# Mixer A's queries and keys: token tiles multiplied as they lie, blocks ordered after the rotary embedding, whole rows stored

## The chip, the core and the metric

The program runs on one core of a Trainium2 chip. The metric is the device time of one execution in microseconds (us), as the median of several runs. PE is the matrix engine (TensorE), DVE the vector engine, ACT the scalar engine, POOL is GpSimd, and SP issues most of the DMA transfers. Each engine works through its own instructions in a fixed order that was set when the program was built; an instruction that waits holds up everything behind it on its engine.

## What is computed

One decoder layer over 2048 tokens of width 1024. The part that matters here makes the rotated queries and keys of mixer A:

```python
h = rmsnorm(x, g_attn[l])
proj = jnp.einsum('bsd,de->bse', h, w_in[l]) + b_in[l]
qa, ka, va, qb, kb, vb = jnp.split(proj, splits, axis=-1)
...
def sliding_window_sink_gqa(q, k, v, sinks):
    S = q.shape[1]
    q, k = rope(q, S), rope(k, S)
    o, _ = banded_attention(q.transpose(0, 2, 1, 3), k.transpose(0, 2, 1, 3),
                            v.transpose(0, 2, 1, 3), WINDOW_A - 1, sinks=sinks)
```

`qa` has 8 heads of 64 (512 columns), `ka` 2 heads (128 columns): five column tiles of 128. `rope` multiplies each feature by the cosine of its token's angle and adds its partner feature, 32 places away, times the sine. Mixer A then attends in blocks of 128 neighbouring tokens. Mixer B attends to the same normalised input with other projections and needs a bias table for each of its 8 heads; behind both come the output projection and a gated feed-forward network.

## The kernel before

The kernel holds the normalised input transposed in SBUF, as two parts that sum to it (`hh` and the rest `hl`), features on partitions and tokens along the row. The tokens lie sorted by their remainder modulo 16: column `n` of `hh` is a token of remainder class `n // 128`, and the 128 places in a class run in steps of 16 tokens. Mixer B wants that order. Mixer A wants blocks of neighbouring tokens.

`project` works in three stretches. First it normalises the input and makes the values (to about 148 us of the profiled execution). Then, in lines 280 to 314, it makes mixer A's queries and keys: for each of five column tiles `c` (0 to 3 queries, 4 the keys) and four token tiles `t` of 512, `gemm` issues 24 matmuls into one PSUM bank (8 chunks of features by 3 products of parts). These 20 units are called groups here, g0 to g19 in the order in which they run, and the stretch the rotary stretch. With `natural=True`, line 174 picks the 512 tokens of four blocks out of `hh`: 64 pieces of 8 neighbouring elements each, the pieces 128 elements apart. Third come mixer A's attention and mixer B's projections, interleaved; these call `gemm` with `natural=False`, which reads 512 neighbouring elements.

What follows a group's matmuls is a chain over three engines. Lines 300 to 303 copy the four quarters of the bank, crosswise, into `t1`, by turns on DVE (L303) and ACT (L301), each waiting for the one before; L305 (DVE) adds the bias and multiplies by the cosine, the last to read the bank; L306 (DVE) does the same with the sine; L307 (POOL) adds; L309 (ACT) and L310 (DVE) split the sum into two parts `hia`; line 311 stores it as two DMAs from SP, one for each head. `t1`, `t2` and `hia` have two buffers each.

Between these stand mixer B's bias tables (`bias_tables`), two steps for each of eight heads. `rows` multiplies three small matmuls into PSUM (L381), copies them out on ACT (L382, tile `lt`, two buffers) and stores them (L383, `Ls`). `table` loads them back skewed (L387, L389, L392: `tt`, `n4`, and four loads for `n1`), reorders them on DVE (L393, L394) and stores the table (L396, `Ts`). `tt`, `n4` and `n1` have one buffer each.

PSUM has 8 banks, and all results of the rotary stretch, those of `gemm` and the three of each `rows`, share one ring of them (`ps2`, 8 buffers).

The order of the instructions on every engine is made by a scheduler when the kernel is built: it goes by the data, the buffers and its own estimate of durations. A buffer or an address that is used again makes the new user wait for the last one. After the rotary stretch its SBUF pools are freed, and the tiles of the third stretch (the masks, keys, queries, scores `t`, probabilities `p` and transposed probabilities `hl` of mixer A, `hi` of mixer B's projections) lie on the same addresses.

Of the kernel before, what the change touches and what calls it, by code (L numbers as in the profile page):

```python
# [43 lines left out]
def shape_constants():  # L44
# [3 lines left out]
    res = np.array(RES)  # L48
    tok = (n // 128) * 128 + (n % 8) * 16 + res[(n % 128) // 8]
    ang = tok.astype(np.float32)[None, :] * inv[:, None]  # L50
# [97 lines left out]
def project(tc, es, ident, half, x, g_attn, w_in, b_in, sinks, rel, rope, mask_a, onehot, sc):  # L148
# [18 lines left out]

    def gemm(ps, w, t, natural, tag="mm"):
        acc = ps.tile([P, 512], F32, tag=tag, name="acc")
        n = 0  # L170
        for k in range(KC):
            for a, h in ((w[0], hh), (w[0], hl), (w[1], hh)):
                if natural:
                    mv = h[:, k, :].rearrange("p (r jj j a) -> p jj j r a", r=16, jj=4, j=4)[:, t]
                else:
                    mv = h[:, k, t * 512:(t + 1) * 512]
                nc.tensor.matmul(acc, a[:, k, :], mv, start=(n == 0), stop=(n == 3 * KC - 1))  # L177
                n += 1
        return acc
# [100 lines left out]
    with ExitStack() as ex:  # L280
        ps = ex.enter_context(tc.tile_pool(name="ps2", bufs=8, space=PSUM, reuse_waits="tile"))
        rp = ex.enter_context(tc.tile_pool(name="r1", bufs=2, reuse_waits="tile"))
        rc = ex.enter_context(tc.tile_pool(name="r2", bufs=1, reuse_waits="tile"))
# [7 lines left out]
        bias = bias_tables(tc, ex, ps, rel, onehot, sc)  # L291
        for c in range(5):
            w = load_w(c * P)
            for t in range(NT):
                cols = slice(t * 512, (t + 1) * 512)
                acc = gemm(ps, w, t, True)
                t1 = rp.tile([P, 512], F32, tag="t1", name="t1")
                for q4 in range(4):
                    d, s4 = t1[q4 * 32:(q4 + 1) * 32, :], acc[(q4 ^ 1) * 32:((q4 ^ 1) + 1) * 32, :]
                    if q4 % 2:  # L300
                        nc.scalar.copy(d, s4)  # L301
                    else:
                        nc.vector.tensor_copy(d, s4)  # L303
                t2 = rp.tile([P, 512], F32, tag="t2", name="t2")
                nc.vector.scalar_tensor_tensor(t2, acc, bcol[:, c:c + 1], tab[:, 0, cols], op0=ALU.add, op1=ALU.mult)  # L305
                nc.vector.scalar_tensor_tensor(t1, t1, bsw[:, c:c + 1], tab[:, 1, cols], op0=ALU.add, op1=ALU.mult)  # L306
                nc.gpsimd.tensor_add(t2, t2, t1)  # L307
                hi = rp.tile([P, 2, 512], F32R, tag="hi", name="hia")
                nc.scalar.copy(hi[:, 0], t2)  # L309
                nc.vector.tensor_sub(hi[:, 1], t2, hi[:, 0].bitcast(F32))  # L310
                store_heads(sc.qA if c < 4 else sc.kA, 2 * c if c < 4 else 0, hi, cols)
                n = c * NT + t - 2
                if 0 <= n < 2 * NH:
                    bias(n // NH, n % NH)


    with ExitStack() as ex:
# [5 lines left out]
        def proj_b(todo, ps=ps, tag="mm"):  # L323
            nonlocal w
            for c0, c, t in todo:
                if t == 0:
                    w = load_w(c0 + c * P)
                bc = bcol[:, c0 // P + c:c0 // P + c + 1]
                acc = gemm(ps, w, t, False, tag)
                hi = ev.tile([P, 2, 512], F32R, tag="hi", name="hi")  # L330
# [17 lines left out]
def bias_tables(tc, es, ps, rel, onehot, sc):  # L348
# [15 lines left out]
    for b in range(3):  # L364
        o32 = bw.tile([P, 384], F32, tag="lt", name="o32")
        nc.sync.dma_start(o32, onehot[:, b, :])
# [8 lines left out]
    def rows(h):  # L375
        lw = bw.tile([P, P], F32R, tag="lw", name="lw")
        nc.vector.tensor_scalar(out=lw, in0=ones, scalar1=rhi[:, h:h + 1].bitcast(F32), scalar2=None, op0=ALU.mult)
        lt = bw.tile([P, 3, 384], F32, tag="lt", name="lt")
        for b in range(3):
# [917 lines left out]
```

## Time and profile before

| | us |
|---|---|
| median of 3 runs | 2406.85 (2405.19 to 2408.16) |
| the profiled execution | 2404.51 |
| its span on the core | 2402.7 |
| PE busy in it | 2300.4 (96%) |
| DVE busy | 1604.5 (67%) |
| ACT busy | 1054.1 (44%) |

In the rotary stretch and up to the first matmuls of attention (about 148 to 304 us) PE is without a pause but for the waits shown in the rows; the granted clock of PE is 1.00 of full speed there. The chain that ended last is PE for 51% of the span. In the views, a row of an engine gives the idle time before an instruction or a group of them and what ended it. SPq rows are the issuing of DMAs; the transfers themselves run later.

### The profile page before, as it was taken

What the parts mean: (1) busy time and instruction counts of PE and PEld (TensorE: products, weight loads), DVE (VectorE), ACT (ScalarE), POOL (GpSimd) and SP (SyncE); (2) the same over time, 40 slices, a digit from 0 to 9 for tenths busy, and PEclk for the clock granted to TensorE, in tenths of its full rate; (3) what the DMA queues carried; (4) which work ended last, traced back from release to release, by engine and by line L of the source; (5) the groups of instructions that cost most, each with busy time, mean ns of one, the idle gap of its engine ahead of it and who ended that gap; (6) DMA issues with size and microseconds to landing.
All of it is one profiled execution on the core that took longest, in us unless ns stands there. A gap on an engine that the chain in (4) does not pass through costs nothing.

```text
span 2402.7 us, 33903 instructions
## 1 busy us (share of the span) xinstructions
PE 2300.4 (96%) x11765; PEld 1947.0 (81%) x11765; DVE 1604.5 (67%) x3151; ACT 1054.1 (44%) x2371; POOL 468.1 (19%) x418
## 2 busy tenths in 40 slices
PE   7999999997999889897999999899999999999998
PEld 7987788886999878785888888678888878888887
DVE  5335655447999977668877776786666746557555
ACT  5323355453898862336332323342332324444442
POOL 2211211111111010113232232423232330000000
PEclk9999999998999999998999999999999999999999
DMA  7666566659988687755544544333232339768651
GB/s 220 202 189 215 159 188 173 165 157 239 222 222 219 174 244 199 241 171 203 196 155 148 175 149 167 127 127 110 91 120 92 106 115 399 240 198 283 205 189 71
DMA packets 284156, 436.21 MB, mean 182 GB/s; under 512 B 24448, under 2 KB 153088, under 8 KB 278480
## 3 DMA queue, kind: packets, MB, share of 16 engines
q1 hardware_dynamic: 279968, 423.41, 57.5%
q0 software_dynamic: 3728, 10.30, 1.5%
q8 instruction: 93, 1.52, 0.3%
q14 instruction: 79, 0.65, 0.1%
q10 hardware_dynamic: 288, 0.33, 0.0%
HBM read 286.50 MB, written 147.46 MB: 181 GB/s over the span
## 4 chain that ended last, share of the span: by engine, by line
PE 51%; DVE 5%; DMA 4%; issue 1%; POOL 0%; ACT 0%; SPq 0%; DVEq 0%; POOLq 0%; ACTq 0%
PE bY L1225 7%; PE Yu L1031 7%; PE Yg L1031 6%; PE bZ L1225 5%; PE bX L1225 5%; PE Xu L1031 4%; PE Zu L1031 4%; PE Zg L1031 4%; PE Xg L1031 4%; PE acco L893 3%; DMA ob<-oB 1%; DVE wl L998 1%; DMA draw<-in_w_down_dram 1%; DVE xs L915 1%; DMA hraw<-hT 0%
## 5 line engine op out<-in xcount | busy, mean ns | idle before, releaser
L1178 DVE TENSOR_TENSOR o<-r,o 128x1024 fp32r<-128x1024 f32 x154 | 191.2, 1252 | 131.9 <-ACT o L1177 124.1
L1177 ACT CAST o<-r 128x1024 fp32r<-128x1024 f32 x154 | 162.2, 1054 | 225.0 <-DMA r<-in_w_down_dram 50.8
L996 ACT CAST wh<-T 128x512 fp32r<-128x512 f32 x176 | 107.2, 621 | 250.1 <-PE Yu L1031 80.5
L1125 POOL TENSOR_TENSOR c<-c,c 128x512 f32<-128x512 f32 x66 | 105.2, 1594 | 567.9 <-DVE c L1049 389.4
L476 DVE TENSOR_TENSOR hl<-pt,hl 128x512 fp32r<-128x512 f32 (+1 forms) x224 | 145.6, 657 | 81.9 <-ACT hl L475 81.4
L451 ACT ACTIVATE p<-t,m 128x256 f32<-128x256 f32 (+1 forms) x384 | 177.4, 480 | 18.0 <-DVE m L676 18.0
L1225 PE MATMUL bY<-o 128*128 128x512 f32 x792 | 180.5, 389 | 0.0
L1225 PEld LDWEIGHTS bY<-o 128*128 128x128 f32 x792 | 148.6, 188 | 30.9
L177 PE MATMUL acc<-hh,wh 128*128 128x512 f32 x416 | 170.0, 409 | 0.7 <-DVE vt L247 0.7
L177 PE MATMUL acc<-hh,wl 128*128 128x512 f32 x416 | 170.4, 410 | 0.0
L177 PE MATMUL acc<-hl,wh 128*128 128x512 f32 x416 | 169.9, 408 | 0.0
L893 PE MATMUL acco<-woh,oT 128*128 128x512 f32 x512 | 163.4, 397 | 3.7 <-ACT oT L864 3.4
L998 DVE TENSOR_TENSOR wl<-T,wh 128x512 fp32r<-128x512 f32 x176 | 153.2, 882 | 0.3
L494 PE MATMUL o<-hl,v 128*128 128x128 f32 (+1 forms) x816 | 141.8, 294 | 7.2 <-DVE hl L476 5.8
L475 ACT CAST hl<-pt 128x512 fp32r<-128x512 f32 (+1 forms) x224 | 125.3, 569 | 45.2 <-PE pt L470 44.9
L429 PE MATMUL s<-k,q 128*128 128x256 f32 (+1 forms) x768 | 122.1, 290 | 18.7 <-DMA k<-kB 8.8
L470 PE MATMUL pt<-ident,p 128*128 128x128 f32 x848 | 133.7, 279 | 4.8 <-DVE hl L476 2.4
L429 PEld LDWEIGHTS s<-k,q 128*128 128x128 f32 x768 | 100.6, 191 | 26.8 <-DVE nma L566 7.4
L1225 PE MATMUL bX<-o 128*128 128x512 f32 x528 | 120.6, 389 | 1.1 <-DVE o L1178 1.1
L494 PEld LDWEIGHTS o<-hl,v 128*128 128x128 f32 x816 | 111.5, 193 | 12.4 <-DVE hl L476 9.6
L1225 PE MATMUL bZ<-o 128*128 128x512 f32 x528 | 120.3, 389 | 0.0
L893 PEld LDWEIGHTS acco<-woh,oT 128*128 128x128 f32 x512 | 96.8, 189 | 25.4 <-ACT oT L864 4.1
(465 smaller groups left out, 5801.3 us busy)
## 6 DMA issues: line engine op xcount, KB each, us to landing
r<-actS SPq DMA_DIRECT2D x154, 256.0 KB
actS<-c SPq DMA_DIRECT2D x128, 256.0 KB
wraw_g<-in_w_gate_dram SPq DMA_DIRECT2D x44, 512.0 KB
wraw_u<-in_w_up_dram SPq DMA_DIRECT2D x44, 512.0 KB
r<-wT SPq DMA_DIRECT2D x88, 256.0 KB
r<-in_w_down_dram SPq DMA_DIRECT2D x66, 256.0 KB
k<-kB SPq DMA_DIRECT2D x32, 512.0 KB
draw<-in_w_down_dram SPq DMA_DIRECT2D x22, 512.0 KB
```

The source lines that it names most:

```text
L177: nc.tensor.matmul(acc, a[:, k, :], mv, start=(n == 0), stop=(n == 3 * KC - 1))
L429: nc.tensor.matmul(s[:, i, :n], b["q"], b["k"][m], start=(m == 0), stop=(m == 1))
L451: nc.scalar.activation(b["pv"](p[:, i, :n]), b["tv"](b["t"]), AF.Exp, scale=-1.0, bias=nm[:, c:c + 1], accum_out=l[:, c:c + 1])
L470: nc.tensor.transpose(pt[:, sl, :], p[:, i, hfn * P:(hfn + 1) * P], ident)
L476: nc.vector.tensor_sub(lo, pt[:, a:z, :], hi.bitcast(F32))
L494: nc.tensor.matmul(out, v[:, vi, :], mov, start=(first and n == 1), stop=(last and n == 2 * len(jobs)))
L893: nc.tensor.matmul(acc, oT[kk // 2][:, kk % 2, a, i * P:(i + 1) * P], b[:, kk, :], start=(n == 0), stop=(n == 11))
L998: nc.vector.tensor_sub(lo, src, hi.bitcast(F32))
L1031: nc.tensor.matmul(bank, a[:, k], b[:, k], start=(first and m == 0), stop=(m == 11), skip_group_check=not first)
L1177: nc.scalar.copy(o[:, 0], r)
L1178: V.tensor_sub(o[:, 1], r, o[:, 0].bitcast(F32))
L1225: nc.tensor.matmul(bank[i], o[:, u, 0, i * P:(i + 1) * P], o[:, v, 1, :], start=(first and j == 0 and m == 0), stop=(j == NP - 1 and m == ...
```

## The change

The `natural` reading is gone: `gemm` always reads 512 neighbouring columns of `hh`, so a group of the rotary stretch now is four remainder classes and not four blocks. The cosine and sine table comes from the host in the same order. The blocks are made behind the rotary embedding: L308 (ACT) and L309 (DVE; L309 and L310 before) write the two parts through a rearranged view, 64 pieces of 8 elements, into one tile `hia` of 2048 tokens for both parts. This tile has one buffer. It is stored once for each column tile, after the fourth group: two DMAs of 1024 KB in rows of 8 KB, in place of eight of 256 KB in rows of 2 KB. The keys' column tile comes first (4, 0, 1, 2, 3). To make room, `lt` of the bias rows, and `o32` which shares its buffers, have one buffer and not two. The pool of the rotary chain is opened after those of the tables, so its tiles lie elsewhere.

```diff
--- before.py
+++ after.py
@@ -46,7 +46,7 @@
     inv = (150000.0 ** (-np.arange(half) / half)).astype(np.float32)
     n = np.arange(S)
     res = np.array(RES)
-    tok = (n // 128) * 128 + (n % 8) * 16 + res[(n % 128) // 8]
+    tok = (n % 128) * 16 + res[n // 128]
     ang = tok.astype(np.float32)[None, :] * inv[:, None]
     cos = np.cos(ang.astype(np.float64)).astype(np.float32)
     sin = np.sin(ang.astype(np.float64)).astype(np.float32)
@@ -165,16 +165,12 @@
         nc.vector.tensor_sub(wl, raw, wh.bitcast(F32))
         return wh, wl
 
-    def gemm(ps, w, t, natural, tag="mm"):
+    def gemm(ps, w, t, tag="mm"):
         acc = ps.tile([P, 512], F32, tag=tag, name="acc")
         n = 0
         for k in range(KC):
             for a, h in ((w[0], hh), (w[0], hl), (w[1], hh)):
-                if natural:
-                    mv = h[:, k, :].rearrange("p (r jj j a) -> p jj j r a", r=16, jj=4, j=4)[:, t]
-                else:
-                    mv = h[:, k, t * 512:(t + 1) * 512]
-                nc.tensor.matmul(acc, a[:, k, :], mv, start=(n == 0), stop=(n == 3 * KC - 1))
+                nc.tensor.matmul(acc, a[:, k, :], h[:, k, t * 512:(t + 1) * 512], start=(n == 0), stop=(n == 3 * KC - 1))
                 n += 1
         return acc
 
@@ -279,7 +275,6 @@
 
     with ExitStack() as ex:
         ps = ex.enter_context(tc.tile_pool(name="ps2", bufs=8, space=PSUM, reuse_waits="tile"))
-        rp = ex.enter_context(tc.tile_pool(name="r1", bufs=2, reuse_waits="tile"))
         rc = ex.enter_context(tc.tile_pool(name="r2", bufs=1, reuse_waits="tile"))
         tab = rc.tile([P, 2, S], F32, name="tab")
         for t in range(NT):
@@ -289,11 +284,13 @@
         for q4 in range(4):
             nc.vector.tensor_copy(bsw[q4 * 32:(q4 + 1) * 32, :], bcol[(q4 ^ 1) * 32:((q4 ^ 1) + 1) * 32, 0:5])
         bias = bias_tables(tc, ex, ps, rel, onehot, sc)
-        for c in range(5):
+        rp = ex.enter_context(tc.tile_pool(name="r1", bufs=2, reuse_waits="tile"))
+        for n, c in enumerate((4, 0, 1, 2, 3)):
             w = load_w(c * P)
+            hi = rp.tile([P, 2, S], F32R, tag="hi", name="hia", bufs=1)
             for t in range(NT):
                 cols = slice(t * 512, (t + 1) * 512)
-                acc = gemm(ps, w, t, True)
+                acc = gemm(ps, w, t)
                 t1 = rp.tile([P, 512], F32, tag="t1", name="t1")
                 for q4 in range(4):
                     d, s4 = t1[q4 * 32:(q4 + 1) * 32, :], acc[(q4 ^ 1) * 32:((q4 ^ 1) + 1) * 32, :]
@@ -305,13 +302,16 @@
                 nc.vector.scalar_tensor_tensor(t2, acc, bcol[:, c:c + 1], tab[:, 0, cols], op0=ALU.add, op1=ALU.mult)
                 nc.vector.scalar_tensor_tensor(t1, t1, bsw[:, c:c + 1], tab[:, 1, cols], op0=ALU.add, op1=ALU.mult)
                 nc.gpsimd.tensor_add(t2, t2, t1)
-                hi = rp.tile([P, 2, 512], F32R, tag="hi", name="hia")
-                nc.scalar.copy(hi[:, 0], t2)
-                nc.vector.tensor_sub(hi[:, 1], t2, hi[:, 0].bitcast(F32))
-                store_heads(sc.qA if c < 4 else sc.kA, 2 * c if c < 4 else 0, hi, cols)
-                n = c * NT + t - 2
-                if 0 <= n < 2 * NH:
-                    bias(n // NH, n % NH)
+
+                hj = [hi[:, u].rearrange("p (j r a) -> p r j a", j=16, r=16)[:, 4 * t:4 * t + 4] for u in range(2)]
+                t2 = t2.rearrange("p (r j a) -> p r j a", r=4, j=16)
+                nc.scalar.copy(hj[0], t2)
+                nc.vector.tensor_sub(hj[1], t2, hj[0].bitcast(F32))
+                if t == NT - 1:
+                    store_heads(sc.qA if c < 4 else sc.kA, 2 * c if c < 4 else 0, hi, slice(0, S))
+                m = n * NT + t - 2
+                if 0 <= m < 2 * NH:
+                    bias(m // NH, m % NH)
 
 
     with ExitStack() as ex:
@@ -326,7 +326,7 @@
                 if t == 0:
                     w = load_w(c0 + c * P)
                 bc = bcol[:, c0 // P + c:c0 // P + c + 1]
-                acc = gemm(ps, w, t, False, tag)
+                acc = gemm(ps, w, t, tag)
                 hi = ev.tile([P, 2, 512], F32R, tag="hi", name="hi")
                 nc.scalar.activation(hi[:, 0], acc, AF.Identity, bias=bc)
                 nc.vector.scalar_tensor_tensor(hi[:, 1], acc, bc, hi[:, 0].bitcast(F32), op0=ALU.add, op1=ALU.subtract)
@@ -362,7 +362,7 @@
     ones = bp.tile([P, P], F32, name="ones")
     nc.vector.memset(ones, 1.0)
     for b in range(3):
-        o32 = bw.tile([P, 384], F32, tag="lt", name="o32")
+        o32 = bw.tile([P, 384], F32, tag="lt", name="o32", bufs=1)
         nc.sync.dma_start(o32, onehot[:, b, :])
         nc.vector.tensor_copy(ohr[:, b, :], o32)
 
@@ -375,7 +375,7 @@
     def rows(h):
         lw = bw.tile([P, P], F32R, tag="lw", name="lw")
         nc.vector.tensor_scalar(out=lw, in0=ones, scalar1=rhi[:, h:h + 1].bitcast(F32), scalar2=None, op0=ALU.mult)
-        lt = bw.tile([P, 3, 384], F32, tag="lt", name="lt")
+        lt = bw.tile([P, 3, 384], F32, tag="lt", name="lt", bufs=1)
         for b in range(3):
             acc = ps.tile([P, 384], F32, tag="mm", name="accb")
             nc.tensor.matmul(acc, lw, ohr[:, b, :], start=True, stop=True)
```

What moves on the engines is shown at three places. Lines of the kernel after are 4 lower around the stores (L179 for L183) and 1 to 5 lower in the chain (L298, L300, L302, L303, L308, L309 for L301, L303, L305, L306, L309, L310).

The first place is SP in the middle of the bias tables, around the loads of head 1's table (the second uses of `n4`, `tt` and `n1`); a number behind a name tells one buffer's use from another, and in square brackets stands whom the instruction waits for. Before:

```order
L183 DMA qA_60<-hia_1737 64x2x512 [waits DMAHW4_49,DVE_49]
L183 DMA qA_60<-hia_1737 64x2x512 [waits DMAHW5_49]
L396 DMA Ts_68<-tt_2170 128x640 [waits DMAHW6_49,DVE_49]
L389 DMA n4_2223<-Ls_67 128x1x256 [waits DMAHW7_49,DMAHW3_49]
L383 DMA Ls_67<-lt_1854 128x3x384 [waits DMAHW0_49,Activation_49]
L392 DMA n1_2225<-Ls_67 32x1x256 [waits DMAHW1_49]
L392 DMA n1_2225<-Ls_67 32x1x256 [waits DMAHW2_49]
L387 DMA tt_2221<-Ls_67 128x128 [waits DMAHW6_49]
L183 DMA qA_60<-hia_1789 64x2x512 [waits DMAHW4_49,DVE_49]
L183 DMA qA_60<-hia_1789 64x2x512 [waits DMAHW5_49]
L392 DMA n1_2225<-Ls_67 32x1x256
L392 DMA n1_2225<-Ls_67 32x1x256 [waits DMAHW7_49]
```

and after, from the store of head 0's table on:

```order
L396 DMA Ts_68<-tt_2144 128x640 [waits DMAHW0_49,DVE_49]
L389 DMA n4_2196<-Ls_67 128x1x256 [waits DMAHW6_49,DMAHW1_49]
L392 DMA n1_2198<-Ls_67 32x1x256 [waits DMAHW4_49,DMAHW5_49,DMAHW3_49,DMAHW2_49]
L392 DMA n1_2198<-Ls_67 32x1x256 x2
L383 DMA Ls_67<-lt_1843 128x3x384 [waits Activation_49]
L387 DMA tt_2194<-Ls_67 128x128 [waits DMAHW0_49]
L392 DMA n1_2198<-Ls_67 32x1x256 [waits DMAHW7_49]
L179 DMA kA_61<-hia_1625 64x2x2048 [waits DVE_49]
L179 DMA kA_61<-hia_1625 64x2x2048 [waits DMAHW1_49]
L389 DMA n4_2251<-Ls_67 128x1x256 [waits DMAHW5_49,DMAHW2_49]
```

Before, a store of two heads' columns (L183) stands between the loads of one table, after every group; after, the loads follow each other, and only behind the fourth group comes a store, of four times the size.

The second place is DVE at the end of the rotary stretch, from the next weight tile's split (L165) to the first scores of attention (L433). Before:

```order
L165 TENSOR_TENSOR wl1280_3010<-raw1280_3006,wh1280_3008 128x1024 [waits DMAHW6_49,Activation_49]
L310 TENSOR_TENSOR hia_2585<-t2_2581,hia_2585 128x512 [waits DMAHW4_49,DMAHW3_49,Activation_49]
L303 COPY t1_2615<-acc_2590 32x512 [waits Activation_49]
L305 SCALAR_TENSOR_TENSOR t2_2620<-acc_2590,bcol_93,tab_1583 128x512 [waits Activation_49]
L306 SCALAR_TENSOR_TENSOR t1_2615<-t1_2615,bsw_1588,tab_1583 128x512 [waits DVE_49]
L310 TENSOR_TENSOR hia_2624<-t2_2620,hia_2624 128x512 [waits DMAHW6_49,DMAHW5_49,Activation_49]
L507 TENSOR_SCALAR nsnk_2647<-snk_2645 128x8 [waits DMAHW7_49,DMAHW1_49,DMAHW0_49]
L332 SCALAR_TENSOR_TENSOR hi_2703<-acc_2678,bcol_93,hi_2703 128x512 [waits Activation_49]
L332 SCALAR_TENSOR_TENSOR hi_2733<-acc_2708,bcol_93,hi_2733 128x512 [waits Activation_49]
L332 SCALAR_TENSOR_TENSOR hi_2763<-acc_2738,bcol_93,hi_2763 128x512 [waits DMAHW5_49,DMAHW4_49,Activation_49]
L433 ISA t_2810,nma_2649<-s_2809,mska_2643,nsnk_2647 128x128 [waits DMAHW6_49,PE_49]
```

and after:

```order
L165 TENSOR_TENSOR wl1280_2965<-raw1280_2961,wh1280_2963 128x1024 [waits DMAHW2_49,Activation_49]
L300 COPY t1_2571<-acc_2546 32x512 [waits Activation_49]
L309 TENSOR_TENSOR hia_2413<-t2_2540,hia_2413 128x4x16x8 [waits Activation_49]
L302 SCALAR_TENSOR_TENSOR t2_2576<-acc_2546,bcol_93,tab_1580 128x512 [waits Activation_49]
L303 SCALAR_TENSOR_TENSOR t1_2571<-t1_2571,bsw_1585,tab_1580 128x512 [waits DVE_49]
L507 TENSOR_SCALAR nsnk_2602<-snk_2600 128x8 [waits DMAHW7_49,DVE_49]
L309 TENSOR_TENSOR hia_2413<-t2_2576,hia_2413 128x4x16x8 [waits Activation_49]
L332 SCALAR_TENSOR_TENSOR hi_2658<-acc_2633,bcol_93,hi_2658 128x512 [waits Activation_49]
L332 SCALAR_TENSOR_TENSOR hi_2688<-acc_2663,bcol_93,hi_2688 128x512 [waits Activation_49]
L332 SCALAR_TENSOR_TENSOR hi_2718<-acc_2693,bcol_93,hi_2718 128x512 [waits DMAHW7_49,DMAHW0_49,Activation_49]
L433 ISA t_2765,nma_2604<-s_2764,mska_2598,nsnk_2602 128x128 [waits DMAHW4_49,DMAHW6_49,DMAHW3_49,PE_49]
```

The last group's split (L310, now L309) stood ahead of the sinks' negation (L507) and now stands behind it. The first scores' instruction (L433), which writes tile `t`, waited for two semaphores and now for four, three of them of DMA queues: its tile lies where `hia` lay.

The third place is SP, which issues the DMAs, from the last weight tile's load of this stretch to the loads of attention. Before:

```order
L161 DMA raw896_3340<-in_w_in_dram 128x8x128 [waits DMAHW7_49,DVE_49]
L183 DMA kA_61<-hia_2585 64x2x512 [waits DMAHW0_49,DVE_49]
L183 DMA kA_61<-hia_2585 64x2x512 [waits DMAHW1_49]
L537 DMA qa_2806<-qA_60 128x2x512 [waits DMAHW2_49,DVE_49]
L537 DMA qa_2906<-qA_60 128x2x512 [waits DMAHW3_49]
L183 DMA kA_61<-hia_2624 64x2x512 [waits DMAHW4_49,DVE_49]
L183 DMA kA_61<-hia_2624 64x2x512 [waits DMAHW5_49]
L503 DMA mska_2643<-in_mask_a_dram 128x256 [waits DMAHW6_49,DMAHW1_49,DMAHW0_49]
L505 DMA snk_2645<-in_sinks_dram 128x8 [waits DMAHW7_49]
L529 DMA ka0_2798<-kA_61 64x512 [waits DMAHW5_49,DMAHW4_49]
L529 DMA ka0_2798<-kA_61 64x512
L529 DMA ka1_2801<-kA_61 64x512 [waits DMAHW2_49]
```

and after:

```order
L161 DMA raw896_3295<-in_w_in_dram 128x8x128 [waits DMAHW5_49,DMAHW2_49,DVE_49]
L503 DMA mska_2598<-in_mask_a_dram 128x256 [waits DVE_49]
L505 DMA snk_2600<-in_sinks_dram 128x8
L529 DMA ka0_2753<-kA_61 64x512 [waits DMAHW0_49]
L529 DMA ka0_2753<-kA_61 64x512 [waits DMAHW1_49]
L529 DMA ka1_2756<-kA_61 64x512
L179 DMA qA_60<-hia_2413 64x2x2048 [waits DMAHW3_49,DVE_49]
L179 DMA qA_60<-hia_2413 64x2x2048 [waits DMAHW4_49]
L529 DMA ka1_2756<-kA_61 64x512 [waits DMAHW5_49]
L533 DMA va_2759<-vA_64 128x4x128 [waits DMAHW6_49]
```

The keys' last store stood ahead of the mask's load (L503), and the keys' loads (L529) waited for it. Now the last store of the stretch is that of the queries of column tile 3; it stands behind the mask and three of the four key loads, and ahead of the fourth.

## Rows read from the trace of the kernel before

**Rows 1.** The page: the span, and each engine's busy time in it.

```profile
span 2402.7 us, 33903 instructions
...
PE 2300.4 (96%) x11765; PEld 1947.0 (81%) x11765; DVE 1604.5 (67%) x3151; ACT 1054.1 (44%) x2371; POOL 468.1 (19%) x418
```

**Rows 2.** Windows, L177 alone: rotary groups, then mixer B's (from:to, length, busy, counts).

```profile
218.00:280.00 62.00, 62.00 (x237) 45.74 (x237) 1.00 0.61 175
281.20:302.40 21.20, 21.20 (x95) 17.57 (x94) 1.00 0.62 174
```

**Rows 3.** Waits of PE, 148 to 304: engine line waited for, us, times, longest.

```profile
PE accb L381 <- DVE ohr L367: 1.2, 1, 1.2
PE accb L381 <- DVE t L305: 0.9, 1, 0.9
```

**Rows 4.** Timeline of PE at attention's start: start, us, engine line, idle before.

```profile
302.82 0.30 PE L429 MATMUL s<-ka,qa 128*128 128x128 f32 x1
303.83 1.09 PE L429 MATMUL s<-ka,qa 128*128 128x128 f32 x7 [0.71 <-DMA ka<-kA]
```

**Rows 5.** Waits of DVE, 170 to 250.

```profile
DVE tt L394 <- DMA n<-Ls: 9.9, 6, 3.6
DVE tt L393 <- DMA n<-Ls: 8.5, 3, 3.7
DVE tt L393 <- DMA Ts<-tt: 5.9, 4, 3.2
```

**Rows 6.** Timeline of DVE: last table copies of heads 0, 3, 4, 7; L305 of g8.

```profile
181.88 0.40 DVE L394 COPY tt<-n 128x256 f32<-128x256 f32 x1
...
214.97 0.40 DVE L394 COPY tt<-n 128x256 f32<-128x256 f32 x1 [1.05 <-DMA n<-Ls]
...
222.90 0.40 DVE L394 COPY tt<-n 128x256 f32<-128x256 f32 x1 [0.95 <-DMA n<-Ls]
223.34 0.75 DVE L305 SCALAR_TENSOR_TENSOR t<-acc,bcol,tab 128x512 f32<-128x512 f32 x1
...
248.04 0.41 DVE L394 COPY tt<-n 128x256 f32<-128x256 f32 x1
```

**Rows 7.** Lines of DVE, 148 to 295: the chain's steps, busy and mean ns.

```profile
L303 DVE COPY t<-acc 32x512 f32<-32x512 f32 x40 | 27.6, 689 | 11.6 <-ACT t L301 5.8 <-PE acc L177 4.9
L305 DVE SCALAR_TENSOR_TENSOR t<-acc,bcol,tab 128x512 f32<-128x512 f32 x20 | 15.0, 751 | 5.3 <-ACT t L301 5.0
...
L310 DVE TENSOR_TENSOR hia<-t,hia 128x512 fp32r<-128x512 f32 x20 | 13.8, 689 | 10.3 <-ACT hia L309 10.1
```

**Rows 8.** Lines of ACT, 148 to 295.

```profile
L301 ACT COPY t<-acc 32x512 f32<-32x512 f32 x40 | 23.1, 578 | 53.0 <-DVE t L303 52.2
L309 ACT CAST hia<-t 128x512 fp32r<-128x512 f32 x20 | 12.4, 621 | 30.6 <-POOL t L307 30.0
```

**Rows 9.** Timeline of DVE: the last group's end, the sinks, the first scores.

```profile
290.32 0.74 DVE L306 SCALAR_TENSOR_TENSOR t<-t,bsw,tab 128x512 f32<-128x512 f32 x1
293.20 0.69 DVE L310 TENSOR_TENSOR hia<-t,hia 128x512 fp32r<-128x512 f32 x1 [2.14 <-ACT hia L309]
299.76 0.17 DVE L507 TENSOR_SCALAR nsnk<-snk 128x8 f32<-128x8 f32 x1 [5.87 <-DMA snk<-in_sinks_dram]
...
307.80 0.34 DVE L433 CUSTOM_DVE_ANT_1 t<-s,mska,nsnk 128x128 f32<-128x128 f32 x1
```

**Rows 10.** Timeline of SP: issues of a lone store, the sinks, stores of long rows.

```profile
259.84 1.23 SPq L183 DMA_DIRECT2D qA<-hia  x2
...
295.93 0.94 SPq L505 DMA_DIRECT2D snk<-in_sinks_dram  x1
...
772.64 1.10 SPq L412 DMA_DIRECT2D oB<-raw  x2
```

**Rows 11.** Windows of 1 us; at the end PEclk, DMA share, GB/s.

```profile
261.00:262.00 1.00, 1.00 (x6) 0.72 (x5) 0.82 (x2) 0.97 (x2) 0.00 (x0) 1.00 0.91 193
262.00:263.00 1.00, 1.00 (x5) 0.75 (x4) 0.97 (x2) 0.23 (x1) 0.24 (x1) 1.00 0.93 252
263.00:264.00 1.00, 1.00 (x5) 0.73 (x4) 1.00 (x2) 0.00 (x0) 1.00 (x1) 1.00 0.28 88
...
777.00:778.00 1.00, 1.00 (x12) 1.00 (x11) 1.00 (x7) 1.00 (x5) 0.00 (x0) 1.00 1.09 432
```

**Rows 12.** Line 769: a DVE copy that writes pieces of 8 elements.

```profile
L769 DVE COPY raw<-o x32: 680/685/692, 603.6 to 858.1; 128x512 f32<-128x512 f32 x32
```

## The prediction

> **What bounds the kernel now.** I read the page first: PE is busy for 96% of the span [rows 1], so time is won where PE works less or waits less, and lost where it waits more. Then the windows of line 177, the one line that all of `gemm` has. Its matmuls have one shape, but between 218 and 280 us, where only rotary groups run, 237 of them fill 62.0 us, one every 0.2616 us; between 281.2 and 302.4, where mixer B's projections run, 94 or 95 fill 21.2 us, one every 0.2255 us if 94 are taken [rows 2]. [...] What differs is the reading: pieces of 8 elements, 128 apart, against 512 neighbours. The rotary stretch has 480 matmuls of the slow kind.
>
> Third, the waits of PE. From 148 to 304 us it waits little, once for the bias rows' table and once for a bank that L305 had still to read [rows 3], and at the start of attention 0.71 us for the keys that had just been stored [rows 4]. It looks as if only PE counted here. The timeline of DVE says otherwise. The last rotary matmul starts at 280.6 us, but the last group's L306 starts at 290.32 and its split at 293.20 [rows 9]: the chain behind PE is some 10 us late at the end. From 170 us on its stalls are not PE's: DVE stands 24.3 us waiting for the loads and stores of mixer B's tables (9.9 + 8.5 + 5.9) [rows 5], with the rotary chain queued behind it. PE covers that lag with 96 projection matmuls of mixer B that need no rotary result, and then meets attention at 302.82 to 303.83 us, when the keys arrive. So PE and the chain end this stretch together, and a gain on PE counts only as far as the chain comes earlier too.
>
> Behind that point PE's work is the same as before and is laid out almost the same, so I take what the start of attention gains or loses for what the kernel gains or loses.
>
> **The matmuls.** 480 × (0.2616 − 0.2255) = 17.3 us less on PE. Alone, this would bring the first scores from 303.83 to about 286.5. The rows say that the scattered reading costs 36 ns a matmul. [...]
>
> **The order made behind the embedding.** L308 and L309 now write pieces of 8 elements. A DVE copy with just such an output takes 685 ns (L769) [rows 12], the split as it was 689 [rows 7], so I take 0 for both engines. No row has ACT writing so; from the same row the bound is 0 to 0.1 us each, 20 times, on an engine that stands idle 83 us in this stretch waiting for DVE and POOL (53.0 + 30.6) [rows 8]: 0 in the sum.
>
> **How fast the chain goes now.** All results share eight PSUM banks. While the bias rows run, each group takes four of them, so group 10 cannot start before group 8's bank is read by L302. From there PE has 14 groups to the first scores (g10 to g19 and four of mixer B), at 24 × 0.2255 = 5.41 us: 75.8 us. So the first scores stand at the end of g8's L302 plus 75.8.
>
> In both orders g8's multiplication stands behind head 4's last table copy; before, that copy is at 222.90 and L305 at 223.34 [rows 6]. A table cannot be copied until the one before it is stored and its own loads have landed, so the heads follow in a cycle: from head 0 (181.88) to head 7 (248.04) 9.45 us on average, from head 0 to 4 10.26, at best 7.93 (214.97 to 222.90) [rows 6]. The slow ones are those where SP also has to issue a rotary store between the loads (1.23 us for a pair [rows 10], and its 512 KB then run ahead of the loads for over 2 us [rows 11]). The change takes 30 of 40 such issues off SP's queue. Against it stand two stores of 2 MB that fall among the tables, and `lt`: with one buffer ACT has to wait until the rows of the head before are stored, and the crosswise copies wait behind it. I estimate this at 1 us on the way to g8, since DVE stands at a table then anyway. For the cycle I take the mean of the best and the average, 8.7. Head 0's table comes three short groups earlier, 3 × 24 × 0.0361 = 2.6 us. Head 4: 181.9 − 2.6 + 4 × 8.7 + 1 = 215.1. Its L302 ends 1.2 later (0.44 behind the copy, 0.75 long): 216.3. First scores: 216.3 + 75.8 = 292.1. With a cycle of 7.93 it would be 289, with 10.26 298.3.
>
> **The one buffer and the long store.** Behind each column tile the split of the next one waits until 2 MB have landed. The queue before shows a lone store of 512 KB in rows of 2 KB: issued from 259.84 [rows 10], moving from 261.0 to 263.3 at 193 to 252 GB/s [rows 11]. For rows of 8 KB the nearest is mixer B's output (L412): 64 partitions, 8 KB each, two halves, issued at 772.64 [rows 10]; where I place it in the queue, the engines move 432 GB/s [rows 11]. The price of 2 MB lies between 2.1 / 420 and 2.1 / 250, that is 5.0 and 8.4 us, plus 1.2 to start and about 0.4 to report: 6.6 to 10.0 us. I take 6.6, since form and row length are those of L412. [...]
>
> While the store runs, DVE has work: the multiplications of the next group (1.5 us), a whole front of the one after (four copies by turns of 689 and 578 ns and two multiplications, 4.3 us with the gaps [rows 7, 8]), and a copy (0.7): 6.5 us. So each tile waits 0.1 us at 6.6 and 3.5 us at 10.0.
>
> **The end.** After head 7's copy (215.1 + 3 × 8.7 = 241.2) the split of g11 ends at about 243. Then come two tiles: the wait of 6.6, and 12.6 us of chain behind it (L308, two splits, the rest of one front, a whole one with the weights' split, and the next one's copies up to the last split), cut at 9.8 in the last tile, where the last L303 ends: 243 + 19.2 + 16.4 = 278.6. The mask lies on the table's address, so SP loads mask and sinks only now; the sinks took 3.8 us from issue to use (295.93 to 299.76) [rows 9, 10] and go out 0.7 behind the mask. The last split now stands behind them: 278.6 + 0.7 + 3.8 + 0.8 = 283.9, the last store lands at 290.6, and the fourth key load, issued behind it, about 1 later: 291.6. This is as late as PE's 292.1, but not later. Queued behind the store on SP are also the values and mixer B's first stores; the third projection's split, and L433 behind it, wait for those, and stood 5 us behind the first scores before (307.80) without holding PE up.
>
> The sum: 303.8 − 292.1 = 11.7 us. I round to 11, for the small stalls that the walk leaves out. Against the profiled execution's own 2404.5 us that is 2393.5; the median of the runs shown lies 2.3 above that execution, so 2396.
>
> **Rivals.**
> - *The chain gains all of it* (chance 0.10): the cycle at its best and PE hardly held, the first scores at 287 to 289: −15 to −17, 2390 to 2392. For it: DMA engines are far from full (share 0.61) [rows 2]. Against: the cycle was at its best once in seven.
> - *Tables no faster than before* (0.20): the cycle stays at 10.26, the first scores at 298.3: −5.5, 2401. For it: the number of table loads is unchanged, and each long store holds up one of them. Against: the loads follow each other now. A little slower still, and the gain is under 0.2%.
> - *The long stores make it slower* (0.17): one mechanism, the landing of 2 MB. At 10.0 us after issue, as the lone store's 250 GB/s gives, the two stores among the tables put 3.4 each on heads 4 to 7 (216.3 becomes 223), and the last three (two waits and the end) another 10.2: the fourth key load lands at 291.6 + 6.8 + 10.2 = 308.6, the first scores with it, +5, 2411.5. It decides from a landing of about 9.1 us on, where five times the excess over 6.6 has eaten the 12 us. For it: the only lone store in the trace. Against: L412. [...]
> [...]
>
> **How the numbers follow.** My forecast has 0.50, with a range of its own of −8 to −14 us, 2393 to 2399. What this kernel's measurement can tell from no change is about 0.2%, 4.8 us: faster is below 2402.0. Faster: 0.50, 0.10, and 0.07 from the tables, which straddle the bound, less 0.02 for the scheduler's small rearrangements far behind, whose waits I took as equal: 0.65. Same: 0.13 of the tables, 0.03 of the reading, 0.04 of the long stores: 0.20. Slower, mostly by 0.2% or a little more: 0.15, from the long stores and those rearrangements. The range takes in the best cycle and most of the slow landing: 2388 to 2410.
>
> **What would show it.** Right: rotary matmuls every 0.226 us; PE waiting for L302 around groups 8 to 10; head 4's copy near 215; the first scores near 292; a split of the first group of a tile waiting for `hia`'s store under 1 us. Wrong: DMA waits of several us ahead of L308, the first scores waiting for the fourth key load, L308 or L309 longer than 0.7 us, or a cycle of over 10 us.

## The result, and the profile after

The changed kernel took 2422.28 us (median of 4, 2419.56 to 2425.59), the kernel before beside it 2406.02 (2402.50 to 2408.16): a ratio of 1.0063, 95% interval 1.0044 to 1.0083. By this ratio it is slower by 15 us, where 11 us less were forecast, and it lies outside the range. The profiled execution has a span of 2420.7 us against 2402.7 [rows 1].

I read the waits of PE first, of the changed kernel, 148 to 304 us, then 300 to 320 (engine and line that waited, what for, us, times, longest):

```profile
PE acc L173 <- DVE t L302: 9.6, 1, 9.6
PE acc L173 <- ACT lt L382: 6.6, 2, 5.8
PE accb L381 <- DVE ohr L367: 1.3, 1, 1.3
...
PE s L429 <- DMA ka<-kA: 10.5, 1, 10.5
```

Where PE had waited some 2 us, and 0.7 for the keys [rows 3, 4], it now waits 17.5 in the stretch and 10.5 for the keys. The timeline of PE (start, us, instruction; in brackets the idle time before it and what ended it) has the first scores 10.26 us later than the 303.83 of before:

```profile
303.35 0.22 PE L429 MATMUL s<-ka,qa 128*128 128x128 f32 x1
314.09 1.20 PE L429 MATMUL s<-ka,qa 128*128 128x128 f32 x4 [10.52 <-DMA ka<-kA]
```

Behind these waits stand the stores of 2 MB. The timelines of SP (issues) and ACT (the cast that next writes the buffer):

```profile
182.96 1.32 SPq L179 DMA_DIRECT2D kA<-hia  x2
...
215.61 1.27 SPq L179 DMA_DIRECT2D qA<-hia  x2
...
249.44 1.29 SPq L179 DMA_DIRECT2D qA<-hia  x2
274.91 1.23 SPq L179 DMA_DIRECT2D qA<-hia  x2
301.15 1.28 SPq L179 DMA_DIRECT2D qA<-hia  x2
302.47 2.62 SPq L529 DMA_DIRECT2D ka<-kA  x1
```

```profile
195.87 1.14 ACT L308 CAST hia<-t 128x512 fp32r<-128x512 f32 x2 [7.12 <-DMA kA<-hia]
...
228.37 1.15 ACT L308 CAST hia<-t 128x512 fp32r<-128x512 f32 x2 [7.20 <-DMA qA<-hia]
...
261.50 1.14 ACT L308 CAST hia<-t 128x512 fp32r<-128x512 f32 x2 [7.91 <-DMA qA<-hia]
286.70 1.14 ACT L308 CAST hia<-t 128x512 fp32r<-128x512 f32 x2 [7.66 <-DMA qA<-hia]
```

From issue to the cast it is 12.9, 12.8, 12.1 and 11.8 us. While the last of these four stores moves, no other transfer does (windows of 1 us: the length, the busy share of PE, PEld, DVE, ACT and POOL, PEld being PE's weight loads; at the end PEclk, DMA share, GB/s):

```profile
276.00:277.00 1.00, 0.00 (x0) 0.00 (x0) 0.97 (x2) 0.00 (x0) 0.51 (x1) 0.50 1.25 262
282.00:283.00 1.00, 1.00 (x3) 0.74 (x3) 0.00 (x0) 0.00 (x0) 0.00 (x0) 0.50 1.12 262
284.00:285.00 1.00, 1.00 (x6) 0.78 (x6) 0.00 (x0) 0.00 (x0) 0.00 (x0) 1.00 1.00 205
```

From 276 to 286 the queue carried 2.11 MB, 211 GB/s, at a share of 95.6% of the 16 engines: the engines are occupied, yet they move half of the 432 GB/s that one window of the kernel before shows [rows 11]. PE's clock shows here too: PE is idle from 270 to 280, and its granted clock is 0.50 from 273 until 283.

The stores also hold up the tables. DVE's last table copies of heads 4, 5 and 7, where [rows 6] had 222.90 and 248.04 for heads 4 and 7:

```profile
216.60 0.41 DVE L394 COPY tt<-n 128x256 f32<-128x256 f32 x1 [1.06 <-DMA n<-Ls]
...
231.80 0.39 DVE L394 COPY tt<-n 128x256 f32<-128x256 f32 x1 [0.48 <-DMA n<-Ls]
...
247.57 0.40 DVE L394 COPY tt<-n 128x256 f32<-128x256 f32 x1 [0.99 <-DMA n<-Ls]
```

Head 4 is 6 us earlier than before; then a store is issued (215.61), the next cycle takes 15.2 us, and by head 7 the lead is gone.

### The profile page after: what moved, and what is told of

It is laid out like the page before. It is cut to its first block, busy times and chain, and to the rows that moved or that the text cites. A ratio compares the mean times of both kernels' runs of the same rounds, so it can differ in the third digit from the quotient of the medians.

```text
span 2420.7 us, 33828 instructions
## 1 busy us (share of the span) xinstructions
PE 2299.3 (95%) x11765; PEld 1957.9 (81%) x11765; DVE 1602.5 (66%) x3151; ACT 1055.3 (44%) x2371; POOL 466.1 (19%) x418
## 4 chain that ended last, share of the span: by engine, by line
PE 51%; DVE 3%; DMA 1%; issue 1%; POOL 0%; ACT 0%; DVEq 0%; POOLq 0%; SPq 0%; ACTq 0%
PE bY L1225 7%; PE Yu L1031 7%; PE Yg L1031 7%; PE bZ L1225 5%; PE bX L1225 5%; PE Xu L1031 5%; PE Zu L1031 5%; PE Xg L1031 4%; PE Zg L1031 4%; PE acco L893 2%; DMA hraw<-hT 1%; DMA ob<-oB 1%; DVE xs L915 0%; DVE wl L998 0%; DVE s L979 0%
## 5 line engine op out<-in xcount | busy, mean ns | idle before, releaser
L173 PE MATMUL acc<-hh,wl 128*128 128x512 f32 x416 | 165.5, 398 | 0.0
L173 PE MATMUL acc<-hl,wh 128*128 128x512 f32 x416 | 165.0, 397 | 0.0
```

What stands on the lines that cost most here:

```text
L173: nc.tensor.matmul(acc, a[:, k, :], h[:, k, t * 512:(t + 1) * 512], start=(n == 0), stop=(n == 3 * KC - 1))
```

## The experiments

**Is it the 64 partitions?** Each half of the store reads partitions 0 to 63 or 64 to 127. The first attempt cut it by part, so that each transfer reads all 128 (the edit in shorthand):

```
-  dst[h + u] "s d n -> d s n"               <- hi[u * 64:u * 64 + 64]
+  [[2*64*S, 2], [S, 64], [1, S]] of dst[h, s]  <- hi[:, s]
```

> The changed kernel, but each 2 MB store is cut by part (all 128 partitions' leading half, then all 128 partitions' rest, 1 MB each, rows of 8 KB) and not by head (64 partitions each). Theory A (the two halves of 64 partitions move one after the other, each at about half of what the queue can carry: 2.1 MB at some 200 GB/s by the windows of the changed kernel, 12 us from issue to the next tile's L308): the store now runs at about 400 GB/s, lands 6.5 to 7.5 us after issue, PE's wait for L302 (9.6 us) and for the fourth key load (10.5) mostly go, and the time is 2395 to 2403. [...] Rival B (any store of this size in rows of 8 KB moves at 200 to 250 GB/s, whichever partitions it comes from): landing stays at 11 to 13 us and the time at 2420 to 2425.

It took 2568.15 us (ratio 1.0679, 1.0661 to 1.0697): a miss of both theories. With each part a tile of its own

> As the run with stores cut by part, and the two parts are tiles of their own, so that the cast of the next tile (L308) waits only for the first part's store, which is issued right behind the cast. Theory A: the first part lands about 4 us after its issue, the second about 7; the wait ahead of L308 falls under 1 us, and the time is 0 to 5 us under that of the run with one tile, 2393 to 2400. Rival B (200 to 250 GB/s whatever the partitions): the first part lands after 6 to 7, the second after 11 to 13, time 2414 to 2422.

it took 2569.15 (1.0666, 1.0651 to 1.0682). A window of the run cut by part, while kA's store (issued at 181.55) moves, and ACT's cast behind it:

```profile
190.00:191.00 1.00, 1.00 (x6) 0.84 (x5) 0.00 (x0) 0.00 (x0) 0.87 (x1) 1.00 0.14 57
```

```profile
225.08 1.14 ACT L312 CAST hia<-t 128x512 fp32r<-128x512 f32 x2 [37.11 <-DMA kA<-hia]
```

A share of 0.14 is what about 2 of 16 engines would give, as many as the outermost dimension of the pattern in HBM is long. The question of the partitions was not answered: the experiment had changed something else. With 64 there, in the changed kernel, the share was 95.6%, and with 128, in the run below, 0.94 to 1.09; that its length sets the number of engines is my reading of these three forms.

The second attempt changes the arrays instead, so that the 128 rows of a part stand together (shorthand; the loads change with it):

```
-  qA [NH, 2, HD, S]                 +  qA [NH // 2, 2, P, S]
-  store_heads(...)                  +  for s in 0, 1:  qA[c][s] <- hi[:, s]
```

> The changed kernel with another layout of the two arrays that the stores fill: the leading parts of a column tile's 128 rows stand together, then the rests, so that each of the two 1 MB transfers reads 128 partitions and its outermost dimension is 128 long (in the run with stores cut by part it was 2 long, and the store ran at 53 GB/s). Each load of queries becomes two, of 64 partitions. Theory A (64 partitions at a time are what held the store to 210 GB/s): it now runs at about 400 GB/s and lands 7 to 8 us after issue, the waits ahead of L308 fall from 7.2 to 7.9 to about 3, the first scores that stood at 314.1 come near 296 to 299, and the time is 2398 to 2406. Rival B (a lone store of this size gets 200 to 250 GB/s from whichever partitions): landing 11 to 13, time 2418 to 2424.

It took 2402.51 us (12 runs, 2394.02 to 2409.94; the profiled one is the fastest): 0.9970 of before (0.9955 to 0.9984), the first version faster than before. SP, ACT, and the windows between:

```profile
259.35 1.05 SPq L312 DMA_DIRECT2D qA<-hia  x2
```

```profile
265.79 0.62 ACT L308 CAST hia<-t 128x512 fp32r<-128x512 f32 x1 [1.58 <-DMA qA<-hia]
```

```profile
260.00:261.00 1.00, 1.00 (x6) 0.83 (x5) 0.97 (x3) 0.00 (x0) 0.00 (x0) 1.00 0.94 393
263.00:264.00 1.00, 1.00 (x7) 0.81 (x6) 0.60 (x1) 0.37 (x1) 0.00 (x0) 1.00 1.09 451
```

The same bytes in the same rows of 8 KB land after 6.4 us at 390 to 450 GB/s (7.8 us for the store before it, which has loads of queries behind it). Theory A stands; the waits ahead of L308 are 0.5 to 2.7 us. PE has one long wait left, for the keys, and its first scores stand at 289.86, 6 to 9 us earlier than I expected:

```profile
283.98 0.26 PE L430 MATMUL s<-ka,qa 128*128 128x128 f32 x1
289.86 1.40 PE L430 MATMUL s<-ka,qa 128*128 128x128 f32 x5 [5.62 <-DMA ka<-kA]
```

With two tiles on top,

> As the run with the layout for 128 partitions, and the leading parts and the rests are tiles of their own, so that the next tile's cast (L308) waits only for the first 1 MB, issued right behind the cast. Theory A: the first part lands about 5 us after its issue, when DVE and ACT still have other work, so the wait ahead of L308 goes under 1 us, and the time is 2 to 6 us under that of the run with one tile, 2393 to 2402. Rival B: first part after 6 to 7, second after 11 to 13, 2412 to 2420.

it took 2404.80 (0.9980, 0.9967 to 0.9993), above what was expected. The waits ahead of L308 went to 0.4 to 2.2, but the first scores stood at 291.27: no gain. PE's one long wait was again that for the keys, 5.8 us.

**Or the two rows of one partition in a transfer?** The halves as the even and the odd partitions, two rows from each as in the changed kernel (hi[b:P:2]):

> As the run with the layout for 128 partitions, but each of the two transfers of a long store reads 64 partitions again, two rows of 8 KB from each, as in the changed kernel; only they are not partitions 0 to 63 and 64 to 127 but the even ones and the odd ones. Theory A (it is the block of 64 neighbouring partitions that has only half of the ways out): the store moves at about 400 GB/s, lands 6.5 to 7.5 us after issue, time 2398 to 2408, as the run with 128 partitions. Rival C (64 partitions at a time, or two rows from one partition, hold it to 210 GB/s wherever the partitions stand): landing 11.5 to 13, time 2418 to 2426. [...]

SP, ACT and a window of it:

```profile
262.33 1.25 SPq L313 DMA_DIRECT2D qA<-hia  x2
```

```profile
269.57 1.14 ACT L308 CAST hia<-t 128x512 fp32r<-128x512 f32 x2 [3.11 <-DMA qA<-hia]
```

```profile
264.00:265.00 1.00, 1.00 (x6) 0.81 (x6) 0.46 (x1) 0.46 (x1) 1.00 (x1) 1.00 1.03 418
```

Landing 7.2 us at 393 to 434 GB/s: it is the 64 neighbouring partitions, not their number or the two rows. The time, 2408.25 (0.9992, 0.9980 to 1.0004), is just past theory A's upper end; the first scores stand at 292.68, and the rest is lost behind the stretch (below).

Both fast runs also have the new arrays in HBM, and neighbouring partitions with these arrays were not run. Two transfers that move alone, both in pieces of 2 KB of rows that follow each other in HBM, speak against the arrays as the cause: L412 of the kernel before, from 64 neighbours, and the store of the layout for 128 partitions on the kernel before (its time is in the table below):

```profile
868.00:869.00 1.00, 1.00 (x12) 1.00 (x11) 0.58 (x2) 1.00 (x5) 0.00 (x0) 1.00 0.94 205
...
252.00:253.00 1.00, 1.00 (x6) 0.74 (x5) 0.56 (x1) 0.40 (x1) 0.00 (x0) 1.00 0.95 358
```

At the same share of the engines 64 neighbours give 205 GB/s, 128 partitions 358.

**Can the halves move side by side?** The second half on ACT's queue (q = nc.scalar if u else nc.sync):

> The changed kernel, with the second half of each long store (partitions 64 to 127) issued on ACT's queue, so that both halves can move at once; arrays and row lengths as in the changed kernel. Theory A (each half alone can use only half of the way out of the on-chip memory): both together move at about 400 GB/s, landing 7 to 8 us after the later issue, time 2399 to 2407. Rival B (the engines' rate for such rows is the bound): the two halves share 200 to 250 GB/s, landing 11 to 13, time 2418 to 2424.

It took 2430.47 (1.0084, 1.0068 to 1.0101), above both ranges. Both halves were issued at 277.51, and the cast behind them came 11.8 us later, as rival B said. The queues' packets, MB and share, 278 to 281 us and 284 to 287 (q10 is ACT's, q1 SP's):

```profile
q10 hardware_dynamic: 64, 0.52, 84.3%
...
q1 hardware_dynamic: 93, 0.76, 106.0%
```

From 278 to 281 only the half on ACT's queue moved, 0.52 MB at a mean of 175 GB/s; from 284 to 287 it was the other, 0.76 MB at 254 GB/s, with 11 small packets (0.00 MB) of the first. So this says nothing against theory A; it says that two queues did not bring the halves together.

**What each part is worth.** The reading alone (the kernel before, moving operand h[:, k, t * 512:(t + 1) * 512]):

> The kernel before with one edit: the rotary groups read their tokens as they lie (512 neighbours). The order of blocks is left out with it, so mixer A gets its queries and keys in another order of tokens; stores and everything else are as before. Theory (the stretch is bound by the chain of embeddings behind the tables, so PE's 17.3 us count only in part): PE waits for L305 or for a bank instead, first scores at 296 to 300, time 2399 to 2404. Rival (PE bounds the stretch, so the reading is worth its full price): first scores near 287, time near 2390.

The changed kernel without it:

> The changed kernel with the scattered reading of the kernel before put back, and so with no order made behind the embedding; the one buffer of 16 KB and the 2 MB stores stay. Theory (the long stores bound the stretch, PE has some 27 us of waits in it that take up the 17.3 us): 2422 to 2429, PE's waits for L302 and for the key load shorter by about what the reading costs. Rival (reading and store add up): 2437 to 2441.

The layout for 128 partitions without it:

> The run with the layout for 128 partitions, with the scattered reading of the kernel before put back (and no order made behind the embedding). Theory (with short landings PE is the bound of the stretch: there it stood only 5.6 us, for the key load, and had its last projection at 283.98): 480 matmuls of 36 ns more put that to 301.3, past the key load's 289.9, so 10 to 12 us more than that run, 2411 to 2417. Rival (the chain of embeddings is the bound, as in the kernel before with the contiguous reading alone, which gained nothing): 0 to 3 us more, 2402 to 2407.

The layout without whole rows, on the kernel before:

> The kernel before, with the layout for 128 partitions alone: each group's store of 512 KB is cut by part and reads 128 partitions, in rows of 2 KB; scattered reading, two buffers of 8 KB and 20 such stores as before. It tells what of the gain of the changed kernel with this layout is due to the layout alone. Theory (stores of 512 KB hide behind two buffers and cost the chain little; the tables' cycle, held by SP's issues, stays): attention starts at 301 to 304, time within 3 us of before. Rival (the layout is what wins, since each store clears the engines for the tables in half the time): attention starts at 295 to 298, time 5 to 8 us less.

| stores | scattered: first scores, median | contiguous: first scores, median |
|---|---|---|
| 512 KB, 64 partitions | 303.83, 2406 to 2411 (before) | 301.69, 2408.92 (1.0002, 0.9991 to 1.0013) |
| 512 KB, 128 partitions | 301.66, 2414.34 (1.0022, 1.0005 to 1.0039) | not run |
| 2 MB, 64 partitions | 314.56, 2429.27 (1.0087, 1.0074 to 1.0101) | 314.09, 2422.28 (the change) |
| 2 MB, 128 partitions | 298.57, 2407.38 (0.9997, 0.9984 to 1.0010) | 289.86, 2402.51 |

The first scores are those of one profiled execution each; a second one of the kernel before has 302.53. No part gains time by itself. The reading alone was to take 2399 to 2404 by my theory and missed that. It brings the first scores only 0.8 to 2.1 us, since the chain behind the tables keeps its pace and PE stands ahead of them. DVE of that run, with the last table copy and the last split 45.2 us apart, and PE:

```profile
245.79 0.38 DVE L394 COPY tt<-n 128x256 f32<-128x256 f32 x1
...
290.96 0.69 DVE L310 TENSOR_TENSOR hia<-t,hia 128x512 fp32r<-128x512 f32 x1 [2.14 <-ACT hia L309]
```

```profile
300.18 0.45 PE L429 MATMUL s<-ka,qa 128*128 128x128 f32 x1 [6.19 <-issue]
```

Before, the copy and the split were as far apart [rows 6, 9]. Without the reading, the changed kernel loses some 6 us more by the ratios, 7 by the medians: a little past the upper end of what was expected and far from the sum of both prices. Its first scores move by only 0.5 us.

In the run with the layout for 128 partitions, with 30 fewer stores on SP and a fast landing, the last table copy comes at 235.61. Only then is PE the bound: with the scattered reading put back PE has no wait for the keys, and the reading is worth 8.7 us of first scores (298.57 to 289.86). The time of that run missed my theory (10 to 12 us more, 2411 to 2417) and lies just past the rival's range. My theory for the layout alone was right on the start of attention and 2 us off in the time.

Three parts of the change were never taken out by themselves: `lt`'s one buffer, for which ACT waits 8.0 us in the changed kernel's stretch (L382 behind `Ls`; none before), the order of the column tiles, and the place of the chain's pool.

**The keys behind the last store.** With that store on ACT's queue (q = nc.scalar if c == 3 else nc.sync):

> The run with the layout for 128 partitions, with the last column tile's store issued on ACT's queue, so that the last two key loads need not stand behind it on SP. Theory: the keys are there when PE is done with mixer B's projections, PE's wait for them falls from 5.6 to 0 to 2 us, time 2 to 5 us less, 2397 to 2401. Rival (the DMA engines take ACT's queue first, as in the run with two queues): the wait stays at 4 to 6 us, 2401 to 2405.

It took 2400.89 (0.9965, 0.9951 to 0.9978): about 21 us under the changed kernel, and the lowest median here, though not clear of the run without this edit (0.9955 to 0.9984). The wait fell to 3.0 and the first scores to 286.52, between theory and rival.

**What is lost behind the stretch.** The two profiled executions differ by 10.8 us through mixer A's attention, and by more from mixer B's on. SP's first load for mixer B and its first output store, in the kernel before, the changed kernel, and the kernel before with the reading alone:

```profile
545.65 0.63 SPq L604 DMA_DIRECT2D q<-qB  x1
...
633.19 1.39 SPq L412 DMA_DIRECT2D oB<-raw  x2
```

```profile
556.42 0.64 SPq L604 DMA_DIRECT2D q<-qB  x1
...
647.55 1.30 SPq L412 DMA_DIRECT2D oB<-raw  x2
```

```profile
545.44 0.64 SPq L604 DMA_DIRECT2D q<-qB  x1
...
639.68 1.22 SPq L412 DMA_DIRECT2D oB<-raw  x2
```

So +10.77 became +14.36, and −0.21 became +6.49 in a kernel that has the same work there as before. The windows of PE in this passage (busy time, matmuls, PEclk, DMA share, GB/s) show where the time goes, in the kernel before and in the one with the reading alone:

```profile
555.00:565.00 10.00, 4.08 (x18) 0.50 1.07 307
565.00:575.00 10.00, 8.41 (x50) 0.85 1.04 282
585.00:595.00 10.00, 8.07 (x54) 1.00 1.17 228
```

```profile
555.00:565.00 10.00, 4.48 (x20) 0.53 1.07 300
565.00:575.00 10.00, 8.89 (x38) 0.50 1.07 305
585.00:595.00 10.00, 9.76 (x43) 0.50 1.15 224
```

PE stands 7 us for mixer B's keys in these three, and its granted clock falls to 0.50. In the kernel before it was back at 568, after 13 us; with the reading alone at 597, after some 41, and at 0.50 PE gets through 43 matmuls in 10 us, where it does 54 at 1.00. The changed kernel is another case: its clock was back by 574, and fell a second time behind no long wait, PE having been busy for most of the 10 us before:

```profile
576.00:586.00 10.00, 7.70 (x51) 1.00 1.04 312
586.00:596.00 10.00, 9.51 (x43) 0.55 1.12 255
```

From 586 to 626 it was 0.55 to 0.92. A second profile of the kernel before was to tell whether the first was short by luck:

> The kernel before, unchanged, for a second profile. Theory (part of the 18 us between the two profiled executions is the passage from mixer A's attention to mixer B's, which was short in the execution that was profiled): attention starts at 303.8 within 1 us, and mixer B's attention comes 2 to 7 us later than in the first profile. Rival (the passage is lengthened by the change itself): all within 1 us.

It was not: 2403.26 us, first scores 1.3 us earlier (the rival said within 1), and the passage as long as in the first. From SP's first load for mixer B to its first output store the two profiles of the kernel before take 87.5 and 87.4 us; the changed kernel takes 91.1, and the other runs 86.8 to 98.2. So I cannot say that the change plays no part in the 3.6 us of the passage. That the clock is lower in the two longer passages shown here is seen; what lets it fall again, or return sooner or later, stays open, and so does the cause of the last 3.6 of the 18.0 us, which come later.

## Why the prediction was wrong

The step that failed is the store's price: "I take 6.6, since form and row length are those of L412". From issue to the next cast it measured 11.8 to 12.9. The row behind it, 432 GB/s [rows 11], is one microsecond in which L412's store was mixed with value loads. From 772 to 782 us the queue moved 2.5 MB, of which L412's are 1.05, and the row says nothing of the store's own rate. The row that did was the lone store beside it, 193 to 252 GB/s [rows 11], also from 64 partitions; I kept it as the far end. Of the two terms that I added to the moving itself, the rows show the 1.2 to start (issue at 259.84, moving from 261.0 [rows 10, 11]); the 0.4 to report is shown by no run, and in the changed kernel's store issued at 274.91 nothing moves from 286.0 on, while the cast starts at 286.70: 0.7.

- The matmuls: right. In the changed kernel 64 fill 289 to 303 us, 80 or 81 fill 230 to 248; there is no other kind left. For a scattered reading that costs nothing, to which the chances give 0.03, no run speaks: the rows have 0.2616 us a matmul against 0.2255 [rows 2].
- The order behind the embedding: right. L308 620 ns (L309 before: 621), L309 689 (689).
- Head 4's copy at 215.1: 216.60, but from a head 0 at 176.42, not 179.3, and with a long store on the way: two errors that cancel, so this near hit is luck. Cycles without a store took 7.7 to 8.5 us, the two with a long store 15.8 and 15.2, for which a mean of 8.7 had no room. Head 7's copy came at 247.57, not 241.2: 6.4 us. The "best" cycle of 7.93 was misread too: [rows 6] leave out heads 5 and 6, whose last copies in the kernel before stand 6.21 us apart:

```profile
234.15 0.91 DVE L394 COPY tt<-n 128x256 f32<-128x256 f32 x1 [0.78 <-DMA n<-Ls]
...
240.36 0.91 DVE L394 COPY tt<-n 128x256 f32<-128x256 f32 x1 [0.48 <-DMA n<-Ls]
```

- The two tile waits: 12.1 and 11.8 us from store to cast in place of 6.6: 5.5 and 5.2. The work from the cast on, in the tile between (13.4, said 12.6) and in the last (10.6, said 9.8): 0.8 each.
- The end: mask and sinks 1.4 less than said; last store and key load 12.9 in place of 7.7: 5.2.
- Together 6.4 + 5.5 + 5.2 + 0.8 + 0.8 − 1.4 + 5.2 = 22.5, and 291.6 + 22.5 is the 314.1 measured. The waits of 5.5, 5.2 and 5.2 are the landing. The 6.4 among the tables hangs on it as well: with the landing of 128 partitions head 7's copy came 12.0 us earlier, at 235.61.
- The rival "long stores make it slower" (0.17) was the mechanism, and the landing lies past its point of 9.1 us. Its own size, 10.0, was still too small.
- "Laid out almost the same" behind the stretch: not so; 7.2 of the 18.0 us came there.

With about the landing that I took (6.4 to 7.8 us in the run with 128 partitions), the first scores came at 289.86, behind the key load as said, where 291.6 was forecast. The path held; that the number came so near is in part luck. Head 7's copy stood at 235.61 there, 5.6 us ahead of the walk's 241.2, and from it to the first scores were 54.3 us, where the walk has 50.4.

## What to carry to other kernels

Price a transfer by a row in which it moves alone, and ask which partitions it touches: here 64 neighbours stored at 211 GB/s, 128 partitions, or 64 spread over all, at some 400. Before a transfer is re-cut, look at the outermost dimension of its pattern in HBM: with a length of 2 the store ran here at 49 to 57 GB/s, a share of 0.12 to 0.14 of the 16 engines. Where several stages keep pace with one another, one part alone tells little of the whole: the reading brought the first scores 0.5, 0.8 to 2.1, or 8.7 us, by what stood beside it.

## What was not expected of the hardware

- Transfers of 1 MB with an outermost dimension of 2 ran at 49 to 57 GB/s, at a share of 0.12 to 0.14, about 2 of 16 engines.
- Halves issued at one time on two queues moved one after the other (from 278 to 281 us 0.52 MB on ACT's queue alone, from 284 to 287 0.76 MB on SP's).
- Around a wait of 7 us the granted clock stood at half for 13 us in one kernel and 41 in another that does the same there, and the passage differs by 6.7 us; in a third it fell again without such a wait. Runs of one kernel spread more widely (2394 to 2410); that this is the reason was not tested.
